# A transpose of 8192 x 8192 floats: who tells that a chunk is copied, and who waits for the gather

## The chip, the cores and the metric

The kernel runs on one core of a Trainium2 chip. A core has engines that work side by side, each with its own queue of instructions in order: TensorE (PE; its weight loads are listed as PEld), VectorE (DVE), ScalarE (ACT), GpSimd (POOL) and SyncE (SP), which here issues all transfers. They meet only through semaphores: an instruction waits until a counter has a value, another adds to it when it is done. Sixteen DMA engines move data between the chip's main memory and the on-chip memory (SBUF). TensorE writes only to PSUM, and VectorE and ScalarE read it from there.

The metric is the time of one execution on the device, in microseconds (us).

## The reference

```python
def setup_inputs():
    return {"x": np.random.randn(8192, 8192).astype(np.float32)}

def reference(x):
    return np.transpose(x)
```

Nothing is computed: 268 MB are read and 268 MB are written, in another order.

## The kernel before

**Chunks.** The input is taken in 128 chunks (T), each 128 rows by 4096 columns (J), 2 MiB. The first 64 (CH) cover the left half of the columns, the others the right half. A chunk has 16 pieces (NR) of 256 columns (PIECE). TensorE transposes a piece as two 128 x 128 matmuls against an identity, every second column into each, so that 32 matmuls make a chunk. The first 8 pieces go to one half of PSUM, `pss[0]`, which ScalarE empties, the others to `pss[1]`, which VectorE empties.

**A diagonal order.** A store is to write long rows of the output, so it needs 128 columns from each of 16 chunks. Store `w` takes from chunk `t` the one piece that belongs to it; chunk `t` is the last to give a piece to store `t`. That last piece is copied from PSUM directly to its place in `arena` (the direct copy). It lies with ScalarE where t mod 16 is under 8, otherwise with VectorE. All other pieces wait in `slots`, and when chunk `t` comes, VectorE collects the 15 older ones for store `t` from `slots` into `arena`: that is the *gather* (L240 to L263, its copies are L256). It runs ahead of the copies of chunk `t` on VectorE's queue, and its place in `arena` is free only when an older store has landed; there is room for two full stores. Only after the gather of `t` may the copies of `t` overwrite `slots`, since they reuse its places.

**The order on SyncE.** Store t-1, load t+2, store t, load t+3 and so on, in one queue. Three load buffers exist, so load t+3 waits until TensorE has transposed chunk t (`s_pe`). A store waits for the direct copy (`s_xa` or `s_xv`), which stands behind the gather.

**TensorE** runs the chunks in two loops and a rest: chunks 0 to 11 (E = 12), 12 to 125 (LAST = 126), 126 and 127. In the second loop it waits at a chunk's start for both halves of PSUM (`s_free[0]` and `s_free[1]`), runs two wide matmuls of the identity that nobody reads (L360; the profile has each as two), waits for `s_go` and for the load, and transposes (L366). After every four pieces it adds to `s_pe`.

**ScalarE's pacing.** From chunk 24 (CALM) to 125, ScalarE waits for the load, runs two copies of the identity over `pss[0]` (REST = 2, L401), and only then adds to `s_go`. In chunks 12 to 23 it adds to `s_go` at once.

**Who tells what in before.** In `copies(t)` (L265 to L302) each of the two engines waits for the gather (`s_g`), then for the transposes of each run of pieces (`s_pe`), copies the run (L294), and its last copy adds to its own `s_cp`. It then waits for that and adds to `s_free`, which lets TensorE have the half again. The gather waits for both `s_cp`.

## Time and profile before

| | |
|---|---|
| median of 3 runs | 1285.86 us (1265.3 to 1289.19) |
| the profiled execution | 1273.26 us |
| its span, first to last instruction | 1271.5 us |
| PE busy | 861.4 us, 68% |
| DVE busy | 615.1 us, 48% |
| ACT busy | 638.9 us, 50% |
| bytes moved | 537.07 MB, mean 422 GB/s |

The page divides the span into 40 slices and gives for each the busy share of an engine and the rate of the transfers. Its groups of instructions name line, engine, operation and tile, the time of one and the idle time before. "ps" is PSUM. A wait is put down to what came last. PEclk is the clock that TensorE was granted, as a share of the full one.

### The profile page before, as it was taken

To read this page: it belongs to the slowest core of one execution; us is meant where nothing else is said; L and a number is where in the kernel's file an instruction comes from. 1 tells how busy PE (TensorE), PEld (TensorE's weight loads), DVE (VectorE), ACT (ScalarE), POOL (GpSimd) and SP (SyncE) were. 2 spreads that over 40 slices of the span, in tenths; PEclk is the share of its full clock that TensorE was granted. 3 is DMA by queue.
4 is the path that set the end of the run, shared out by engine and by line. 5 is a ranking of instruction groups with operands and counts; after the bars stand their busy time and mean duration, and the time that the engine had idled before them with its cause. 6 is when DMAs were issued, how large, how long until landed. Compare 5 with 4: busy or idle time off the path is not lost. (4 is left out here: it accounts for less than half of the span.)

```text
span 1271.5 us, 12053 instructions
## 1 busy us (share of the span) xinstructions
PE 861.4 (68%) x4552; PEld 655.3 (52%) x4552; DVE 615.1 (48%) x715; ACT 638.9 (50%) x606; POOL 0.7 (0%) x6
## 2 busy tenths in 40 slices
PE   6766767777667766777767777667767667767630
PEld 5755645555545555555555555545555555455420
DVE  3554554455444454444545444554445545445481
ACT  2321224556565566555655565565655656555510
POOL 0000000000000000000000000000000000000000
PEclk9898887889898889888898888988898988889875
DMA  9999999999999999999999999999999999999998
GB/s 387 425 425 426 426 428 426 431 431 430 432 429 431 433 430 430 430 432 421 416 428 428 431 430 431 430 431 432 415 429 430 421 409 404 423 430 432 405 400 335
DMA packets 41332, 537.07 MB, mean 422 GB/s; under 512 B 4576, under 2 KB 5216, under 8 KB 8288
## 3 DMA queue, kind: packets, MB, share of 16 engines
q1 hardware_dynamic: 41312, 536.89, 99.8%
q14 instruction: 18, 0.15, 0.0%
q8 instruction: 2, 0.03, 0.0%
HBM read 268.44 MB, written 268.44 MB: 422 GB/s over the span
## 5 line engine op out<-in xcount | busy, mean ns | idle before, releaser
L366 PEld LDWEIGHTS ps<-ident,arena 128*128 128x128 f32 x4096 | 565.0, 212 | 238.2 <-issue 238.1
L366 PE MATMUL ps<-ident,arena 128*128 128x128 f32 x4096 | 579.9, 306 | 119.9 <-PEq L363 119.1
L256 DVE COPY arena<-slots 128x2048 f32<-128x2048 f32 (+7 forms) x316 | 304.3, 1012 | 483.3 <-DMA out_dram<-arena 473.7
L360 PE MATMUL ps<-ident 128*128 128x512 f32 x456 | 287.5, 764 | 242.2 <-PEq L358 242.2
L401 ACT COPY ps<-ident 128x2048 f32<-128x2048 f32 x204 | 381.4, 1869 | 52.8 <-DMA arena<-in_x_dram 49.0
L294 ACT COPY slots<-ps 128x1024 f32<-128x1024 f32 (+2 forms) x335 | 238.6, 781 | 252.2 <-DVE arena L256 220.8
L294 DVE COPY slots<-ps 128x512 f32<-128x512 f32 (+2 forms) x336 | 289.3, 913 | 64.7 <-PE ps L366 63.5
L360 PEld LDWEIGHTS ps<-ident 128*128 128x128 f32 x456 | 90.3, 219 | 329.8 <-issue 329.8
L294 ACT COPY arena<-ps 128x256 f32<-128x256 f32 x66 | 24.5, 372 | 277.8 <-DVE arena L256 223.4
L294 DVE COPY arena<-ps 128x256 f32<-128x256 f32 x63 | 26.8, 425 | 86.1 <-PE ps L366 85.2
L294 ACT ACT_TABLE_LOAD x1 | 1.3, 1283 | 1.0 <-SPq L148 1.0
L338 POOL TENSOR_SCALAR_AFFINE_SELECT ident<-ident 128x128 f32<-128x128 f32 x1 | 0.3, 292 | 0.2 <-POOL ident L336 0.2
L336 POOL MEMSET ident<- 128x128 f32 x1 | 0.2, 204 | 0.5 <-SPq L148 0.5
L443 POOL MEMSET const-bfloat16-1.0<- 128x1 bf16 x1 | 0.1, 101 | 0.0
L443 POOL MEMSET const-uint8-127<- 128x1 uint8 x1 | 0.1, 101 | 0.0
L443 POOL MEMSET const-float32-0.0<- 128x1 f32 x1 | 0.1, 98 | 0.2 <-issue 0.2
L443 POOL MEMSET const-float32-1.0<- 128x1 f32 x1 | 0.1, 98 | 0.0
## 6 DMA issues: line engine op xcount, KB each, us to landing
arena<-in_x_dram SPq DMA_DIRECT2D x128, 2048.0 KB, 20.3
out_dram<-arena SPq DMA_DIRECT2D x98, 2048.0 KB, 16.7
out_dram<-arena SPq DMA_DIRECT2D x4, 1920.0 KB, 12.4
out_dram<-arena SPq DMA_DIRECT2D x4, 1792.0 KB, 13.2
out_dram<-arena SPq DMA_DIRECT2D x4, 1664.0 KB, 13.9
out_dram<-arena SPq DMA_DIRECT2D x4, 1536.0 KB, 13.9
out_dram<-arena SPq DMA_DIRECT2D x4, 1408.0 KB, 12.6
out_dram<-arena SPq DMA_DIRECT2D x4, 1280.0 KB, 12.9
```

Of the source, the lines that this page charges most:

```text
L256: cp = nc.vector.tensor_copy(out=ap(arena, do, [[P, len(v)], [dist, B], [1, P]]), in_=ap(slots, so, [[gap, len(v)], [P, B], [1, P]]),)
L294: cp = eng.copy(out=dst, in_=i) if e == 0 else eng.tensor_copy(out=dst, in_=i)
L336: nc.gpsimd.memset(ident, 0.0).then_inc(s_id, 1)
L338: nc.gpsimd.affine_select(out=ident, in_=ident, compare_op=mybir.AluOpType.not_equal, fill=1.0, base=0, pattern=[[-1, P]], channel_multipl ...
L360: nc.tensor.matmul(out=pss[1][:, :4 * P], lhsT=ident, rhs=four, start=True, stop=True)
L366: tr = nc.tensor.transpose(pss[h][:, (u * B + b) * P:(u * B + b + 1) * P], arena[:, q + b:q + PIECE - B + b + 1:B], ident,)
L401: cp = nc.scalar.copy(out=pss[0].rearrange("p (k i) -> p k i", i=P), in_=ap(ident, 0, [[0, J // 2 // P], [1, P]]))
L443: nc = _bacc.Bacc("TRN2", target_bir_lowering=False, num_devices=1)
```

## The change

For chunks 11 to 124 (`told`), the engines' last copies add to `s_free` directly, without `s_cp` and without the wait and the separate addition. TensorE, once it has seen both `s_free` at the start of the next chunk, adds to a new semaphore, `s_seen`. Whoever needs to know that such a chunk is copied waits for `s_seen`: the gather (now only ahead of its last copy, which alone takes pieces of the newest chunk), and ScalarE ahead of its pacing copies, which overwrite `pss[0]`.

For chunks 12 to 125 VectorE's copies no longer wait for `s_g`. ScalarE, when the gather has ended, adds to a new semaphore `s_gd`, and TensorE waits for it between the first 8 pieces of the chunk and the second 8. In these chunks VectorE's neighbouring pieces are copied in one instruction even where they come from different groups of four; such a copy waits for the last group. A wait for a group that an earlier wait covered is left out. The last wait of the kernel, for the last store's semaphore, goes from SyncE to VectorE.

```diff
+        def told(t):
+            return E - 1 <= t < LAST - 1
+
+        def wait_copied(eng, k, t):
+            if told(t):
+                eng.wait_ge(s_seen, t - E + 2)
+            else:
+                eng.wait_ge(s_cp[k], copied_by[k, t])
...
-            if runs:
-                for k in range(2):
-                    nc.vector.wait_ge(s_cp[k], upto)
             for v in runs:
+                if v is runs[-1]:
+                    for k in range(2 if upto == T else 1):
+                        wait_copied(nc.vector, k, upto - 1)
...
                 need = max(ready[w] for w in (t, T) if w in ready and direct(w, t))
-                if need:
+                after = E <= t < LAST
+                if after and e == 0:
+                    nc.scalar.sem_inc(s_gd, 1).wait_op(s_g, need, "sem-ge")
+                elif need and not after:
                     eng.wait_ge(s_g, need)
...
                 runs = runs_of(
-                    cells_, lambda a, b: None if None in a + b or a[3] != b[3] else b[2] - a[2]
+                    cells_, lambda a, b: None if None in a + b or (a[3] != b[3] and not (after and e == 1)) else b[2] - a[2]
                 )
-                runs.sort(key=lambda v: v[0][1] != t)
+                runs.sort(key=lambda v: (v[0][1] != t, v[-1][3]))
+                seen = -1
                 for v in runs:
-                    g, w, o, n = v[0]
-                    eng.wait_ge(s_pe, 4 * t + n + 1)
+                    g, w, o, _ = v[0]
+                    n = v[-1][3]
+                    if not after or n > seen:
+                        eng.wait_ge(s_pe, 4 * t + n + 1)
+                        seen = n
...
+                if told(t):
+                    cp.then_inc(s_free[e], 1)
+                    continue
                 cp.then_inc(s_cp[e], 1)
+                copied[e] += 1
+                copied_by[e, t] = copied[e]
                 if t < T - 1:
-                    eng.wait_ge(s_cp[e], t + 1)
+                    eng.wait_ge(s_cp[e], copied[e])
                     eng.sem_inc(s_free[e], 1)
...
                         nc.tensor.sem_inc(s_free[1], -1).wait_op(s_free[1], 1, "sem-ge")
+                        nc.tensor.sem_inc(s_seen, 1)
                         for _ in range(IDLE):
...
+                if g == NR // 2 and E <= t < LAST:
+                    nc.tensor.sem_inc(s_gd, -1).wait_op(s_gd, 1, "sem-ge")
...
                     else:
+                        wait_copied(nc.scalar, 0, u - 1)
                         nc.scalar.wait_ge(s_ld[home["L", u]], 16)
...
         for k in range(2 * W - 1):
-            nc.sync.wait_ge(s_st[k], stored[k])
+            (nc.vector if k == lane(order[-1][1]) else nc.sync).wait_ge(s_st[k], stored[k])
```

More of the change, by code (lines that the diff above doesn't have):

```diff
@@ L163 @@
         s_rest = nc.alloc_semaphore("s_rest")
+        s_seen = nc.alloc_semaphore("s_seen")
+        s_gd = nc.alloc_semaphore("s_gd")
         s_x = [nc.alloc_semaphore("s_xa"), nc.alloc_semaphore("s_xv")]
@@ L172 @@
         shut = [0, 0]
+        copied = [0, 0]
+        copied_by = {}
+        def told(t):
[5 more added lines that the diff above has]
+                eng.wait_ge(s_cp[k], copied_by[k, t])
         REST = 2
@@ L308, in store @@
                 if w == T:
-                    nc.sync.wait_ge(s_cp[0], T)
+                    wait_copied(nc.sync, 0, T - 1)
                 nc.sync.wait_ge(s_g, ready[w])
```

## The prediction

> **What bounds the kernel now.** The page first: span, DMA row, queue.

> ```profile
> span 1271.5 us, 12053 instructions
> ...
> DMA  9999999999999999999999999999999999999998
> GB/s 387 425 425 426 426 428 426 431 431 430 432 429 431 433 430 430 430 432 421 416 428 428 431 430 431 430 431 432 415 429 430 421 409 404 423 430 432 405 400 335
> ...
> q1 hardware_dynamic: 41312, 536.89, 99.8%
> ```

> All compute engines are half idle, the DMA engines never are: about 430 GB/s in nearly every slice. One chunk is a 2 MiB load and a 2 MiB store, 4.19 MB, so 9.8 us per chunk at that rate. Next, how deep the DMA queue stands: the issues by size with their median time to landing, at the start (the first load, nothing ahead of it) and in mid-run (950 to 970 us).

> ```profile
> arena<-in_x_dram SPq DMA_DIRECT2D x1, 2048.0 KB, 7.4
> ...
> out_dram<-arena SPq DMA_DIRECT2D x2, 2048.0 KB, 16.7
> arena<-in_x_dram SPq DMA_DIRECT2D x2, 2048.0 KB, 21.0
> ```

> A load alone lands after 7.4 us; in mid-run a store takes 16.7 and a load 21.0, so 9 to 14 us of each is queueing. A handful of microseconds of delay before an issue only shortens the queue. The change can hurt only by making the compute loop of a chunk longer than 9.8 us. So the loop has to be read: the waits between 200 and 1200 us, then the timeline of two chunks (columns: start, us, engine, line, operation; in brackets the idle time before and its releaser).

> ```profile
> DVE arena L256 <- DMA out_dram<-arena: 422.7, 101, 5.9
> ...
> ACT ps L401 <- DMA arena<-in_x_dram: 49.0, 97, 1.5
> ```
> ```profile
> 640.03 2.42 DVE L294 COPY slots<-ps 128x1024 f32<-128x1024 f32 x3
> ...
> 642.43 3.77 ACT L401 COPY ps<-ident 128x2048 f32<-128x2048 f32 x2 [0.41 <-DMA arena<-in_x_dram]
> ...
> 642.65 1.96 PE L360 MATMUL ps<-ident 128*128 128x512 f32 x4 [1.92 <-PEq L358]
> ...
> 646.46 5.39 PEld L366 LDWEIGHTS ps<-ident,arena 128*128 128x128 f32 x32 [2.68 <-issue]
> 646.49 5.55 PE L366 MATMUL ps<-ident,arena 128*128 128x128 f32 x32 [1.88 <-PEq L363]
> 647.38 2.43 DVE L256 COPY arena<-slots 128x2048 f32<-128x2048 f32 x3 [4.94 <-DMA out_dram<-arena]
> ...
> 651.03 2.42 DVE L294 COPY slots<-ps 128x1024 f32<-128x1024 f32 x3 [1.21 <-PE ps L366]
> ...
> 652.23 3.77 ACT L401 COPY ps<-ident 128x2048 f32<-128x2048 f32 x2 [0.33 <-DMA arena<-in_x_dram]
> ...
> 656.27 3.91 PEld L366 LDWEIGHTS ps<-ident,arena 128*128 128x128 f32 x32 [1.49 <-issue]
> 656.30 4.08 PE L366 MATMUL ps<-ident,arena 128*128 128x128 f32 x32 [0.69 <-PEq L363]
> ```

> A chunk runs so. ScalarE's two pacing copies (L401) start when the load has landed, in 97 of 102 chunks; 3.77 us later they let TensorE go, which transposes for 4.08 to 5.55 us. The gather starts when an old store has landed, ends 2.4 us later, and both engines empty PSUM. Look at the rows at 651.03 and 652.23: VectorE's copies end at 653.45 (651.03 + 2.42), but the next pacing copies began at 652.23. **The pacing runs beside VectorE's copies.** It waits for ScalarE's own copies and the load only.

> **The change, part by part.**

> *Fewer instructions for VectorE.* In the built program its semaphore instructions go from 416 to 60 and its copies from 715 to 623, 448 fewer. VectorE waits 422.7 us for store landings in this stretch, so none of that is on the path by itself: cost 0. Were they all exposed, the chain that ended last gives their size (0.02 and 0.05 us):

> ```profile
> 1200.68 3.65 PE ps L360 x4
> 1204.34 3.83 PE ps L366 x32
> ...
> 1208.26 0.42 DVE arena L294
> ...
> 1210.78 0.02 DVEq L302
> ...
> 1210.89 0.05 DVEq L252
> ```

> At most three or four per chunk, 0.2 us. From the same rows: from the end of the transposes (1208.17) to VectorE's copy is 0.09 us.

> *The pacing copies wait for TensorE's tell.* Chunks no longer count ScalarE's own copies, so before the pacing copies ScalarE waits until `s_seen` counts the chunk before. TensorE adds to it only behind its waits for both `s_free`, so **VectorE's copies too must be done**. Behind this wait stand the pacing copies, behind them `s_go`, behind that all 32 transposes, behind them VectorE's copies, which feed the next tell. That is a closed chain once per chunk, in which nothing overlaps; none of it depended on VectorE's copies before. Its terms:

> 1. VectorE's last copy to the pacing copies. Not in the trace: it is two hops, VectorE to TensorE to ScalarE. One hop is 0.09 (above); two, VectorE by its own semaphore to TensorE, are 642.45 to 642.65, 0.20. I take 0.20; bounds 0.09 and 0.47 (0.20 plus the hop of point 3).
> 2. Pacing: 3.77.
> 3. Pacing's end to the first transpose: 656.00 to 656.27, 0.27. TensorE's idle matmuls (1.96 us above, 3.65 in the row at 1200.68) run beside the pacing.
> 4. Transposes: 4.08 at full clock, 5.55 with a half-speed stretch inside. The granted clock of the stage is 0.88, and 4.08 / 0.88 = 4.64:

> ```profile
> core 0: us, PE busy (x) PEld busy (x) DVE busy (x) ACT busy (x) POOL busy (x), PEclk, DMA share, GB/s
> ...
> 200.40:1198.10 997.70, 705.84 (x3636) 523.91 (x3636) 482.88 (x559) 579.26 (x515) 0.00 (x0) 0.88 1.01 427
> ```

> 5. Transposes' end to VectorE: 0.09.
> 6. What VectorE still has to copy then, by form:

> ```profile
> L294 DVE COPY slots<-ps 128x1024 f32<-128x1024 f32 x145 | 175.2, 1218 | 30.7 <-PE ps L366 29.9
> ...
> L294 DVE COPY slots<-ps 128x512 f32<-128x512 f32 x96 | 62.9, 683 | 29.7 <-PE ps L366 29.5
> L294 DVE COPY slots<-ps 128x768 f32<-128x768 f32 x47 | 44.6, 950 | 4.3 <-PE ps L366 4.1
> ```

> 0.267 us per piece of 256, on a base of 0.15. Its copies are merged now, and a merged copy waits for its last group of transposes, mostly the chunk's last. By t mod 16: for 0 to 3 a last copy of 6, 6, 5, 4 pieces is left (1.75, 1.75, 1.49, 1.22; lengths without a row go by that slope); for 4 to 7 and 12 to 15 all eight pieces (2.42, as in the row at 640.03); for 8 to 11 7, 6, 5, 4 pieces (2.02, 1.75, 1.49, 1.22). Mean 2.00; bounds 1.22 and 2.42.

> Sum: 0.20 + 3.77 + 0.27 + 4.64 + 0.09 + 2.00 = **10.97 us per chunk**. Now the period of before:

> ```profile
> L401 ACT COPY ps<-ident x204: 1869/1869/1871, 200.4 to 1200.0; 128x2048 f32<-128x2048 f32 x102
> ```

> 102 pairs, the last pair starting one copy before 1200.0, at 1198.1: 997.7 / 101 = 9.88 us. The chain is 1.09 us longer, for 101 periods: **+110 us**.

> *TensorE waits for the gather in mid-chunk* (`s_gd`). Behind it are the second eight pieces, VectorE's copies, and for t mod 16 of 8 and more the store. In the new loop the gather can run right after VectorE's last copy and ends 2.4 us later, while TensorE reaches mid-chunk 0.20 + 3.77 + 0.27 + 2.3 = 6.5 us after it. Covered by the pacing if the store before last landed within 4.1 us of that copy's end. The latest stores (t mod 16 from 12) go out 0.09 + 0.42 us after the transposes, 2.0 before VectorE's last copy ends; even at 16.7 us they land 14.7 after that end, and 10.97 + 4.1 = 15.1 is allowed. The queue will be emptier, so cost 0. The next load goes out at the end of the transposes and is wanted some 24 us later; 21.0 holds. From t = 12 to 23 there is no pacing; the chain is 0.20 + 1.96 to 3.65 + 4.64 + 0.09 + 2.00, 8.9 to 10.6, about the 9.8 of the DMA: 0, bounds 0 and +10.

> *The end.* The last wait on VectorE instead of SyncE: 0. With a shorter DMA queue at the last load the flush may start with less backlog: 0, bounds -7 and 0.

> The profiled execution took 1273.26, 1.8 around its span, at the lower side of the three runs (1265.3 to 1289.19). 1273 + 110 = **1383 us**, 7.6% over the median of 1285.86. Those runs differ by 1.9%, so 2% is about what a measurement tells from no change.

> [...] Windows of 3.41 us around a drop of the clock:

> ```profile
> 678.53:681.95 3.42, 1.59 (x14) 1.43 (x13) 3.09 (x4) 2.17 (x3) 0.00 (x0) 1.00 1.03 436
> 681.95:685.36 3.41, 3.41 (x4) 0.96 (x4) 0.00 (x0) 3.38 (x2) 0.00 (x0) 0.50 1.00 426
> ```

> TensorE idle for 1.83 us of one window was at half clock in the next. The new loop idles it about 2.4 us during VectorE's copies and 2.2 us between the idle matmuls and the transposes, so drops go on, and 0.88 is kept. [...]

> **Rivals.**

> - *Full clock.* Transposes of 4.08: the chain is 10.41, 0.53 over 9.88, +54 us: **1327**. For it: runs of 4.08. Against: the window rows.
> - *DMA stays the bound* (the other side). If the chain is under 9.8 us, the tell comes while the load is still on its way and all is hidden: **1273**, at best some microseconds less. It decides at 9.88: terms 4 and 6 at 4.08 and 1.22 with one hop give 9.52, which two of sixteen chunks reach. It needs all terms at their lower ends.
> - *The store loop binds.* If stores kept landing after 16.7 us, two buffers give 2 x period = 16.7 + 2.4 + 0.4 for half the chunks, about 1.2 more for a quarter and 2.4 more for a quarter: 20.4 / 2 = 10.2, +32: **1305**. Against: 16.7 is queueing, which goes when the queue drains.
> - *The clock falls further.* Every chunk at 5.55: 11.88, +202: **1475**.
> - *The change doesn't do as it says*, the tell coming early: not possible, it stands behind both waits in TensorE's queue.

> **How the numbers follow.** Forecast (1340 to 1425) 0.78; full clock 0.08; DMA bound 0.06; store loop 0.03; lower clock 0.03; faster by over 2% 0.02 (under 1260 means 13 of the 23 us by which the span exceeds 536.89 MB at 430 GB/s). Within 2% are the DMA and store cases, 0.09; slower 0.89. Hop and clock bounds (0.83 to full) around 1383 and the full-clock case give the range 1320 to 1425, with 0.86 of the chance.

> **What would show it.** ScalarE's idle time before L401 released by TensorE's queue instead of the load, some 2 to 3 us in nearly every chunk; L401's first and last start some 1110 us apart instead of 999.6; GB/s near 382 in slices 8 to 37 (4.19 MB per 10.97 us); stores landing well under 16.7 us; VectorE's copies ending after the transposes and before the gather. Wrong it is if L401 still waits for the load, or if the gather ends after mid-chunk.

## The result and the profile after

The changed kernel takes 1363.35 us (median of 6 runs, 1353.6 to 1373.3) against 1268.86 us before (6 runs): a ratio of 1.0762, 95% interval 1.0696 to 1.0829. All ratios here leave out executions over 1.5% longer than the fastest of the same kernel, among them two of these six of before, 1285.86 and 1289.19 us. The change makes the kernel slower by 7 to 8%. The profiled execution took 1373.3 us, the longest of the six; it is the one whose lines follow.

The page: span, transfers, the queue, the pacing copies (now L432) and the stores.

```profile
span 1371.5 us, 11822 instructions
...
DMA  9999999999999999999999999989999999999999
GB/s 388 426 427 430 426 430 430 393 369 418 367 359 367 372 424 391 365 406 352 410 398 366 386 370 417 413 345 390 360 410 400 360 412 368 405 413 355 379 370 395
...
q1 hardware_dynamic: 41312, 536.89, 96.8%
...
L432 ACT COPY ps<-ident 128x2048 f32<-128x2048 f32 x204 | 381.4, 1870 | 315.2 <-PEq L386 312.0
...
out_dram<-arena SPq DMA_DIRECT2D x98, 2048.0 KB, 7.6
```

Behind the first slice and up to the seventh (240 us) the rate is as before, about 430 GB/s. From the eighth on, soon after the pacing has begun, it lies between 345 and 424. A full store lands after 7.6 us (median) where it took 16.7, and the first load of before, with nothing ahead of it, took 7.4: the queue of transfers is nearly empty. The busy row still shows nines, which is a coarse digit; the rate tells the difference. ScalarE's idle time ahead of the pacing was 52.8 us, nearly all of it for loads. It is now 315.2 us, and TensorE's queue (L386 is the tell) ends it.

The waits between 200 and 1300 us, and the timeline of two chunks:

```profile
PE ps L388 <- PEq L385: 235.9, 101, 2.8
...
ACT ps L432 <- PEq L386: 308.4, 101, 4.6
...
PE ps L396 <- PEq L391: 136.0, 101, 2.1
...
DVE arena L270 <- DMA out_dram<-arena: 5.5, 3, 2.7
```
```profile
640.34 2.02 DVE L316 COPY slots<-ps 128x1792 f32<-128x1792 f32 x1
...
642.27 2.35 DVE L270 COPY arena<-slots 128x2048 f32<-128x2048 f32 x2
...
642.63 3.77 ACT L432 COPY ps<-ident 128x2048 f32<-128x2048 f32 x2 [3.62 <-PEq L386]
642.65 1.96 PE L388 MATMUL ps<-ident 128*128 128x512 f32 x4 [2.69 <-PEq L385]
...
646.66 3.91 PEld L396 LDWEIGHTS ps<-ident,arena 128*128 128x128 f32 x32 [2.89 <-issue]
646.69 4.07 PE L396 MATMUL ps<-ident,arena 128*128 128x128 f32 x32 [2.09 <-PEq L391]
...
650.80 1.76 DVE L316 COPY slots<-ps 128x1536 f32<-128x1536 f32 x1 [0.27 <-PE ps L396]
652.48 2.29 DVE L270 COPY arena<-slots 128x2048 f32<-128x2048 f32 x3
...
652.84 3.77 ACT L432 COPY ps<-ident 128x2048 f32<-128x2048 f32 x2 [2.92 <-PEq L386]
```

This is the closed chain, row by row: VectorE's last copy ends at 642.36 (640.34 + 2.02), the pacing begins at 642.63, ends at 646.40, the transposes run from 646.66 to 650.76, VectorE's last copy from 650.80 to 652.56, the next pacing begins at 652.84. That is 10.21 us, with the clock full (PEclk 1.00 from 642.36 to 652.56). Before, the pacing began while VectorE still copied. The gather, which waited for landed stores in 101 chunks, waits in 3 now: the stores are early, the compute is late.

How long the stage lasts:

```profile
L432 ACT COPY ps<-ident x204: 1869/1870/1872, 202.2 to 1306.4; 128x2048 f32<-128x2048 f32 x102
```

The last pair starts one copy before 1306.4, at 1304.5; (1304.5 - 202.2) / 101 = 10.91 us per chunk, against 9.88 before.

### The profile page after: what moved, and what is told of

Its sections match the earlier page's. It is cut to its first block, busy times and chain, and to the rows that moved or that the text cites. A ratio compares the mean times of both kernels' runs of the same rounds, so it can differ in the third digit from the quotient of the medians.

```text
span 1371.5 us, 11822 instructions
## 1 busy us (share of the span) xinstructions
PE 881.0 (64%) x4552; PEld 656.9 (48%) x4552; DVE 603.0 (44%) x623; ACT 642.4 (47%) x606; POOL 0.7 (0%) x6
## 3 DMA queue, kind: packets, MB, share of 16 engines
q1 hardware_dynamic: 41312, 536.89, 96.8%
## 5 line engine op out<-in xcount | busy, mean ns | idle before, releaser
L396 PEld LDWEIGHTS ps<-ident,arena 128*128 128x128 f32 x4096 | 559.1, 211 | 304.6 <-issue 304.6
L432 ACT COPY ps<-ident 128x2048 f32<-128x2048 f32 x204 | 381.4, 1870 | 315.2 <-PEq L386 312.0
L388 PE MATMUL ps<-ident 128*128 128x512 f32 x456 | 304.6, 805 | 267.3 <-PEq L385 267.3
L316 DVE COPY slots<-ps 128x512 f32<-128x512 f32 (+7 forms) x244 | 286.3, 1203 | 346.8 <-PE ps L396 346.8
L316 ACT COPY slots<-ps 128x1024 f32<-128x1024 f32 (+2 forms) x335 | 241.9, 779 | 164.5 <-PE ps L396 148.5
L388 PEld LDWEIGHTS ps<-ident 128*128 128x128 f32 x456 | 97.8, 237 | 364.7 <-issue 364.7
L363 POOL MEMSET ident<- 128x128 f32 x1 | 0.2, 205 | 0.5 <-SPq L148 0.5
## 6 DMA issues: line engine op xcount, KB each, us to landing
arena<-in_x_dram SPq DMA_DIRECT2D x128, 2048.0 KB, 12.0
out_dram<-arena SPq DMA_DIRECT2D x98, 2048.0 KB, 7.6
```

The source lines that it names most:

```text
L316: cp = eng.copy(out=dst, in_=i) if e == 0 else eng.tensor_copy(out=dst, in_=i)
L363: nc.gpsimd.memset(ident, 0.0).then_inc(s_id, 1)
L388: nc.tensor.matmul(out=pss[1][:, :4 * P], lhsT=ident, rhs=four, start=True, stop=True)
L396: tr = nc.tensor.transpose(pss[h][:, (u * B + b) * P:(u * B + b + 1) * P], arena[:, q + b:q + PIECE - B + b + 1:B], ident,)
L432: cp = nc.scalar.copy(out=pss[0].rearrange("p (k i) -> p k i", i=P), in_=ap(ident, 0, [[0, J // 2 // P], [1, P]]))
```

## The experiments

All ratios are to the kernel before, timed on the same chip with it; the intervals are 95%. Where they are named, theory A is the chain through the tell, B the wait for the gather in mid-chunk, C the merged copies.

**The pacing waits for ScalarE's own copies again; all else of the change stays.**

```diff
-                if told(t):
+                if told(t) and e == 1:
                     cp.then_inc(s_free[e], 1)
                     continue
...
-                        wait_copied(nc.scalar, 0, u - 1)
```

> The changed kernel, but ScalarE's pacing waits again for ScalarE's own copies (own semaphore, wait, then the tell to TensorE) and not for TensorE's tell; everything else of the change stays. Theory A (the pacing behind VectorE's copies closes a chain of 10.9 us per chunk): the chain is open again, the loads set the pace, period 9.88 us, ratio to before 0.99 to 1.01. Rival B (TensorE's wait for the gather in mid-chunk is the cause): stays at about 1.075. Rival C (VectorE's merged copies, late to begin, are the cause by themselves): stays at about 1.07.

Measured: 1270.04 us against 1270.76, ratio 1.0008 (0.9976 to 1.0039). With ScalarE's own tell back in place of TensorE's, the whole loss is gone. The load starts the pacing again (waits of this kernel):

```profile
ACT ps L431 <- DMA arena<-in_x_dram: 29.4, 79, 0.7
```

B and C fall as causes by themselves, since the mid-chunk wait and the merged copies are still there. It also says what the rest of the change is worth: 448 fewer instructions for VectorE give no gain that these runs can see.

**The wait of the pacing alone, in the kernel before.**

```diff
                         nc.tensor.sem_inc(s_free[1], -1).wait_op(s_free[1], 1, "sem-ge")
+                        nc.tensor.sem_inc(s_seen, 1)
...
+                        nc.scalar.wait_ge(s_seen, u - E + 1)
                         nc.scalar.wait_ge(s_ld[home["L", u]], 16)
```

> The kernel before, with one part of the change alone: TensorE adds to its tell behind both waits at a chunk's start, and the pacing waits for it. No merged copies, no wait for the gather in mid-chunk, all of VectorE's waits kept. Theory A: the chain is about 0.38 (hop, one more wait of VectorE on itself) + 3.77 + 0.27 + 4.56 + 1.75 (copies of one group of four, all eight for t mod 16 from 12) = 10.7 us, +86 us over 101 periods less about 6 at the end: ratio 1.05 to 1.07. Rivals B and C: 1.00.

Measured: 1348.32 us, ratio 1.0597 (1.0546 to 1.0649). Most of the loss is there with this one part, 78 of 94 us. The wait and the period, from this kernel's profile (L360 is the tell):

```profile
ACT ps L404 <- PEq L360: 283.3, 102, 4.8
...
L404 ACT COPY ps<-ident x204: 1869/1870/1872, 202.3 to 1279.6; 128x2048 f32<-128x2048 f32 x102
```

(1279.6 - 1.9 - 202.3) / 101 = 10.65 us; 10.7 was expected. The 0.26 us up to the 10.91 of the whole change are, in the means of the two traces, 0.22 for VectorE's copies after the transposes (2.04 against 1.82) and 0.09 for the transposes (4.56 against 4.48), less 0.05 for the way from VectorE's last copy to the pacing (0.28 against 0.33).

**The change without the merging of VectorE's copies.**

```diff
-                    cells_, lambda a, b: None if None in a + b or (a[3] != b[3] and not (after and e == 1)) else b[2] - a[2]
+                    cells_, lambda a, b: None if None in a + b or a[3] != b[3] else b[2] - a[2]
```

> The changed kernel without VectorE's merging: copies are cut again where pieces come from different groups of four. Theory A: what is left for VectorE after the transposes falls by 1.0 us for t mod 16 of 4 to 7, by 0.1 to 0.6 for 0, 1, 2, 8, 9, 10, nothing for the others, mean 0.36; -36 us, ratio about 1.045. Rival C (merging is all of it): 1.00. Rival B: 1.075.

Measured: 1336.19 us, ratio 1.051 (1.0461 to 1.0558), 27 us under the changed kernel's median. The ratio that was expected, 1.045, lies just outside the interval.

```profile
L432 ACT COPY ps<-ident x204: 1869/1870/1871, 201.9 to 1268.3; 128x2048 f32<-128x2048 f32 x102
```

(1268.3 - 1.9 - 201.9) / 101 = 10.54 us, 0.37 under the changed kernel, where 0.36 was expected. Not all of that is the merging: over the 102 chunks of the stage, what VectorE still has to do after the transposes falls from 2.04 to 1.75 us, and the transposes themselves are 0.08 shorter in this profile. The 0.29 us of the remainder are 29 us over 101 periods, near the 27 of the medians. For t mod 16 from 4 to 7 the remainder falls from 2.38 to 1.48, 0.9 where 1.0 was expected; for 12 to 15 it stays near 2.5, as the sum had it. The saved instructions made the chain longer: a merged copy waits for its last group.

**The change without the hand-over of the gather's end.**

```diff
-                if after and e == 0:
-                    nc.scalar.sem_inc(s_gd, 1).wait_op(s_g, need, "sem-ge")
-                elif need and not after:
+                if need:
                     eng.wait_ge(s_g, need)
...
-                if g == NR // 2 and E <= t < LAST:
-                    nc.tensor.sem_inc(s_gd, -1).wait_op(s_gd, 1, "sem-ge")
```

> The changed kernel without the hand-over of the gather's end: both engines' copies wait for the gather themselves as before, TensorE doesn't wait in mid-chunk. Theory A: the gather ends 6 us before the transposes do in the changed kernel's profile, so nothing changes, 1.07 to 1.08. Rival B: 1.00.

Measured: 1375.17 us, ratio 1.0806 (1.0719 to 1.0894), not to be told from the 1.0762 of the change. The mid-chunk wait costs nothing there. The rows of the changed kernel show why: the gather that began at 642.27 ends at 644.62, two microseconds before the chunk's first transpose.

**One pacing copy in place of two, in the changed kernel.**

```diff
-        REST = 2
+        REST = 1
```

> The changed kernel with one pacing copy of 1.87 us per chunk in place of two. Theory A: the chain is 10.91 - 1.90 = 9.0 us, shorter than the 9.8 us of the transfers of a chunk; the wait ends before the load lands again, DMA busy share 1.0, ratio to before 0.99 to 1.01. A chain in which the pacing does not stand: 1.07 stays.

Measured: 1269.39 us, ratio 0.9988 (0.9956 to 1.0021). The time came as expected, the wait did not:

```profile
DVE arena L270 <- DMA out_dram<-arena: 303.5, 114, 4.2
ACT ps L432 <- PEq L386: 273.9, 102, 4.3
...
PE ps L396 <- PEq L393: 54.7, 51, 2.3
```
```profile
200.40:1198.10 997.70, 699.09 (x3646) 514.67 (x3646) 486.12 (x482) 393.36 (x416) 0.00 (x0) 0.90 1.01 428
```

In all 102 chunks the tell, not the load, still starts the pacing. But the transfers run at 428 GB/s again, and the loop meets them at another place: VectorE's gather waits for a landed store, 114 times. Behind the gather come ScalarE's copies and TensorE's mid-chunk wait (L393), on which TensorE stood 51 times, and behind the copies of both engines comes the tell. A wait that ends last is not the bound if something ahead of it waits for the transfers.

**Four idle matmuls in place of two, in the changed kernel.**

```diff
-        IDLE = 2
+        IDLE = 4
```

> The changed kernel with four wide idle matmuls (8 in the profile, about 3.9 us) in place of two: they fill TensorE's 2.06 us of idle time between the idle matmuls and the transposes and should end just before the pacing does. If windows with much idle time are what lowers the clock: granted clock well over 0.87, transposes near 4.11 us, chain 10.91 - 0.45 = 10.46 us, -46 us, ratio 1.035 to 1.045. If the clock goes by something else: 1.07 to 1.08, or over it where idle matmuls at half clock outlast the pacing.

Measured: 1375.26 us, ratio 1.0826 (1.0756 to 1.0896): no gain. The clock did rise, from 0.87 in the changed kernel's stage to 0.94 in the window below, and the transposes took 4.22 us in the mean of the 102 chunks, 4.56 in the changed kernel. But the idle matmuls can outlast the pacing, as in this chunk:

```profile
core 0: us, PE busy (x) PEld busy (x) DVE busy (x) ACT busy (x) POOL busy (x), PEclk, DMA share, GB/s
200.40:1198.10 997.70, 759.94 (x3684) 515.50 (x3683) 432.56 (x439) 527.41 (x470) 0.00 (x0) 0.94 0.97 387
```
```profile
644.13 3.77 ACT L432 COPY ps<-ident 128x2048 f32<-128x2048 f32 x2 [3.48 <-PEq L386]
644.15 5.37 PE L388 MATMUL ps<-ident 128*128 128x512 f32 x8 [2.69 <-PEq L385]
```

The idle matmuls take 5.37 us, 1.6 more than the pacing, and run partly at half speed: two of their weight loads begin 0.43 us apart (644.65 and 645.08), as at PEclk 1.00 in the changed kernel (643.15 and 643.58); the next four follow at 0.85 to 0.86 us each, up to 648.49. They hold the transposes up in 36 of the 102 chunks, so that in the mean these begin 0.56 us after the pacing, 0.27 in the changed kernel. Of the 0.35 us by which the transposes are shorter, that takes 0.29. The period is (1306.5 - 1.9 - 209.7) / 101 = 10.84 us, 7 us less over the stage, and the stage begins 7.5 us later (209.7 against 202.2):

```profile
L432 ACT COPY ps<-ident x204: 1869/1870/1872, 209.7 to 1306.5; 128x2048 f32<-128x2048 f32 x102
```

Why the chunks before the pacing take longer was not followed. This run leaves open what a fuller clock is worth, so two more kernels were run, once each and so without an interval.

**Three idle matmuls.**

```diff
-        IDLE = 2
+        IDLE = 3
```

> The changed kernel with three wide idle matmuls (6 in the profile, about 2.9 us at full clock, 5.1 at half): the idle stretch between them and the transposes falls from 2.06 to about 1.1 us and the clock should rise above 0.87; at half clock the idle matmuls outlast the pacing by about 1 us. Chain between 10.4 and 11.0 us, time 1315 to 1375. If the clock goes by something else, 1363.

Measured: 1343.35 us. Granted clock 0.93 in the stage, transposes 4.19 us in the mean.

```profile
L432 ACT COPY ps<-ident x204: 1869/1870/1872, 209.2 to 1277.3; 128x2048 f32<-128x2048 f32 x102
```

(1277.3 - 1.9 - 209.2) / 101 = 10.56 us, 0.35 under the changed kernel; the transposes are 0.37 shorter. The stage is 36 us shorter than the changed kernel's and begins 7 us later, which makes 29 of the 30 us between the two spans (1341.6 and 1371.5).

**No idle matmuls.**

```diff
-        IDLE = 2
+        IDLE = 0
```

> The changed kernel without the idle matmuls: TensorE then idles about 6.4 us between two chunks. If idle time in a window lowers the clock: half speed at the start of every chunk, transposes 5.6 us or more, chain 0.28 + 3.77 + 0.26 + 5.6 + 2.04 = 11.95 us or more, +105 us or more over the changed kernel, time 1465 or more. If the clock goes by something else: 4.57 us stay, about 1363.

Measured: 1520.32 us, 157 over the changed kernel's median.

```profile
L432 ACT COPY ps<-ident x204: 1869/1870/1871, 202.7 to 1452.3; 128x2048 f32<-128x2048 f32 x102
```
```profile
650.26 5.52 PE L396 MATMUL ps<-ident,arena 128*128 128x128 f32 x32 [5.80 <-PEq L391]
```
```profile
202.00:1300.00 1098.00, 531.46 (x2840) 517.28 (x2841) 415.51 (x422) 516.75 (x453) 0.00 (x0) 0.69 0.87 342
```

The fences are the pacing's rows, one chunk's transposes and the stage's window (columns as above) of this kernel: TensorE idles 5.80 us ahead of these transposes, the clock is 0.69, no chunk transposes at full speed, and the mean is 6.01 us. The chain with that term is 0.28 + 3.77 + 0.26 + 6.01 + 2.04 = 12.36; the rows give (1452.3 - 1.9 - 202.7) / 101 = 12.35. The chain is a sum: a term made longer shows in the period in full.

**One pacing copy in the kernel before.**

```diff
-        REST = 2
+        REST = 1
```

> The kernel before with one pacing copy in place of two. Transfers set its pace, the pacing is beside them: ratio 0.995 to 1.005 if nothing else hangs on when TensorE begins; a change over 1% would say that the pacing also sets how the transfers run.

Measured: ratio 1.0031 (0.9979 to 1.0083). In the kernel before, the pacing lies beside the transfers, and its length does not show.

## Why the prediction was right, and where its sizes were off

**What bounds the kernel.** Before, the transfers: right. A shorter chain left no mark: with one pacing copy the ratio is 0.9988 in the changed kernel and 1.0031 in the kernel before. After, the chain: without the wait that closes it the loss is gone (1.0008), and that wait alone brings most of it (78 of 94 us).

**The chain's terms**, forecast and mean of the 102 chunks of the changed kernel's trace:

| term | forecast | measured |
|---|---|---|
| VectorE's last copy to the pacing | 0.20 | 0.28 |
| pacing | 3.77 | 3.77 |
| pacing's end to the first transpose | 0.27 | 0.27 |
| transposes | 4.64 | 4.56 |
| VectorE after the transposes | 2.09 | 2.04 |
| sum | 10.97 | 10.92 |

The mean idle time of ScalarE ahead of the pacing is 308.4 / 101 = 3.1 us, where 2 to 3 was named; the first and last pacing copy are 1104.2 us apart (forecast 1110); the rate in the stage is 387 GB/s (forecast 382):

```profile
200.40:1306.00 1105.60, 731.75 (x3638) 529.87 (x3639) 477.21 (x483) 584.16 (x516) 0.00 (x0) 0.87 0.96 387
```

**The fourth term owes something to luck.** It divides the full-clock time by the mean clock of the stage. In the changed kernel's stage, at 0.87, the same division gives 4.08 / 0.87 = 4.69 where 4.56 was measured; with the wait of the pacing alone, at 0.87 too, 4.48 was measured. The forecast was nearer because it started from the 0.88 of before.

**The end was mis-sized.** It was taken at 0, with bounds -7 and 0; it came near the lower one. The pacing stage is 104.6 us longer (1102.3 against 997.7) and starts 1.8 later (202.2 against 200.4); from its last pair to the end of the span there are 67.0 us (1371.5 - 1304.5) against 73.4 before, so -6.4. Together 100.0, which is the difference of the spans. The forecast had +110: 5 us of the ten are the chain, 6 the end, and the later start takes 2 of them back. No run shows by itself whether the end is shorter for the reason that was named, the shorter queue of transfers.

**The clock in the runs.** The median lies 10 us under the profiled execution, which had a granted clock of 0.867 over its span; the fastest of the six, 1353.6 us, had 0.903. By the fourth term, 4.08 / 0.867 - 4.08 / 0.903 = 0.19 us per chunk, 19 us over 101 periods; the two executions are 19.7 apart. So the spread of the changed kernel's runs goes with TensorE's clock, but a cause is not shown by that: another of the six, also at 0.867, took 1368.44 us, and the division is rough, as said. In the kernel before, the time does not go with the clock: of its runs beside the experiments, two at 0.893 took 1270.39 and 1283.02 us.

**The percentage was luck.** The forecast of 7.6% is the measured one. But both of its parts were too long: 1383 us by 20 (ten in the end and the chain, ten because the sum goes from one profiled execution to another, and this one lies above its median), and the median of before, 1285.86 us, by 17 against that of the six runs. Against the execution that the sum started from, 1273.26 us, the forecast is 8.6%.

**The parts costed at nothing** were right: the mid-chunk wait (the run without it), fewer instructions (the run with the pacing's own wait).

**The rivals.** Full clock, 1327 us, is out: the clock of the stage is 0.87, and 35 of the 102 chunks took about 4.9 us or more for transposes that take 4.1 at full clock. TensorE's longest idle times ahead of a block in the waits above are 2.8 and 2.1 us. Its idle time ahead of the blocks (ended by L385 and L391) adds up to 434.2 us over the run of the changed kernel, 321.6 with four idle matmuls and 714.2 without any; the clock of the stage was 0.87, 0.94 and 0.69. A clock at half in every chunk, 1475 us, is out for the changed kernel: 67 of its chunks took 4.1 to 4.2 us. The store loop is out, since stores land in 7.6 us. DMA as the bound is out, and the run with one pacing copy shows the point from which it would have been in.

```profile
354.84:358.26 3.42, 1.82 (x4) 0.68 (x4) 3.42 (x5) 1.85 (x1) 0.00 (x0) 1.00 1.09 383
358.26:361.67 3.41, 1.32 (x11) 1.22 (x11) 0.21 (x1) 1.89 (x2) 0.00 (x0) 1.00 0.84 336
361.67:365.08 3.41, 3.41 (x19) 3.41 (x18) 0.00 (x0) 1.74 (x4) 0.00 (x0) 0.50 0.83 356
```

TensorE is busy for 0.53 of the first and the clock stays; it is busy for 0.39 of the second, with one gap of 2.1 us, and the third is at half clock. Over the pacing stage of this trace there are 237 windows at full clock, and 69 of them are followed by half clock. In all 69 TensorE was busy for less than 0.48 of the window, and every window under 0.43 was among them; in between, some were and some were not. In the same stage of the kernel before there are 59 drops, all after windows under 0.49. In these two traces, then, a drop goes with the share of one window in which TensorE idles, and not with the length of a gap by itself: in the changed kernel 38 of the 69 drops stand behind a gap under 2.2 us, while 45 windows that a gap of 2.4 us or more reaches into were not followed by one.

**What stays open.** What decides between 0.43 and 0.48 is not shown. No version was found that is faster than both kernels: the one with the pacing's own wait and the one with one pacing copy stand level with the kernel before.

## What to carry to other kernels

Before a wait is exchanged for another that "knows more", ask what the old one did not wait for: here one engine's own copies became both engines', and work that had run side by side became one chain. Add that chain up from one finished copy round to the next and hold it against the period of the bound; idle engines and a full DMA row said nothing on it here (VectorE busy for 44% of the changed kernel's span, nines in its DMA row). Ask too whether the engine on which an instruction is saved had idle time: 448 fewer on VectorE gave no gain here (ratio 1.0008 with the chain open), and a copy merged to save some began later (in the closed chain it cost 0.29 us per chunk).

## What the runs showed of the hardware that was not expected

In the changed kernel the way from VectorE through TensorE's queue to ScalarE took 0.28 us (mean of the stage) from the end of one copy to the start of the next; 0.20 was the estimate.

Matmuls that compute nothing paid for themselves in time in this kernel: without them the kernel took 1520 us (one run), with two per chunk 1363, with three 1343 (one run), with four 1375. The clock rose with each (0.69, 0.87, 0.93, 0.94 in the stage), but four of them, partly at half speed (weight loads 0.85 us apart in place of 0.43), ran 5.37 us in the chunk shown and delayed the transposes that they were to hasten.
